# A top-2 router kernel whose first loads are regrouped: logits first, then x in four pieces, and the early store's rows multiplied second

## The chip, the cores and the metric

One core of a Trainium2 chip runs the program. The metric is the device time of one execution in microseconds (us), given as the median of five runs; beside the runs there is one execution taken by the hardware profiler, and all rows quoted below come from that one. Work on the core is done by engines that run independently: here VectorE (DVE) does all the arithmetic, ScalarE (ACT) computes two sigmoids, and 16 DMA engines move data between the device memory (HBM) and the on-chip memory (SBUF, 128 partitions). A DMA is issued by an instruction on SyncE's queue (SPq) or ScalarE's queue (ACTq) and then runs by itself.

## The reference

```python
x: (16, 1024, 512) float32; router_logits: (16, 1024, 8) float32; k = 2
probs = softmax(router_logits)                  # over the 8 experts
topk_probs = the two largest probs, ascending   # (16, 1024, 2)
topk_probs = topk_probs / sum(topk_probs)
out = x[:, :, None, :] * topk_probs[..., None]  # (16, 1024, 2, 512) float32
```

Each of the 16384 tokens is copied twice, scaled by its two normalized weights. The two weights depend only on the difference of the two largest logits: sigmoid(-d) and sigmoid(d). x is 33.6 MB, the logits 0.5 MB and the output 67.1 MB, 101.2 MB in all.

## The kernel before

The 16384 tokens are cut into two groups, of 65 and 63 tokens per partition (`GROUPS`); a "row" below is one token in each of the 128 partitions, so a row of x is 2 KB per partition and 0.26 MB in all, and a row of output twice that. A DMA over n rows is carried as 128 packets, one for each partition, 8 on each of the 16 DMA engines, so the packet is n x 2 KB for a load and n x 4 KB for a store.

There are two big tiles: `xs` holds a whole group of x (65 rows), `osp` holds 16 rows of output. The rest of a group's output is written over rows of `xs` that are no longer needed (`over`). Eight small tiles and `WA` hold the work on the logits.

The order of DMAs on SyncE's queue is the order of the program, and each instruction there waits in line. In group 0 the loads of x (L112) have 2, 2, 4, 8, 17, 28 and 4 rows; behind the first 16 rows stand the two logits loads (L116 for group 0, L117 for group 1), and `top2_weights` (L27 to L43) computes the weights of all 128 rows at once: eleven VectorE instructions over both groups, then two sigmoids on ScalarE. Then come the multiplies (L128), each followed by the store of its rows (L136):

```python
begin = [(0, e, osp[:, :e]), (e, L - e, osp[:, e:])] if g == 0 else [(0, L, osp)]   # e = 2, L = 16
```

In group 0 the multiplies have 2 rows (into `osp`, stored from ScalarE's queue: the "early store", 1 MB), 14 rows (`osp`), 16 rows (over `xs`), 8 and 8 rows (`osp`), 9 and 8 rows (over `xs`); in group 1 16 rows (`osp`), 16 rows (over `xs`), 8, 8 (`osp`) and 15 rows (over `xs`). All stores but the early one are issued on SyncE's queue. A multiply into `osp` waits until the earlier store out of `osp` has landed, and the loads of group 1 wait until the stores out of `xs` have landed. Waits are written by the framework, which also gives each DMA one of eight completion counters in turn; a DMA that reuses a counter waits for that counter's earlier DMA.

The tiles are placed in SBUF in the order in which the program asks for them. In the built program of before `logits` begins at byte 16512 of each partition, `xs` at 20608, `osp` at 153728, and the small tiles follow.

Of the kernel before, what the change touches and what calls it, by code (L numbers as in the profile page):

```python
# [1 line left out]

# [4 lines left out]

F32 = mybir.dt.float32
ALU = mybir.AluOpType
ACTF = mybir.ActivationFunctionType  # L10
P = 128


def top2_weights(nc, pool, logits, M, E):

    hi, lo, n = None, None, E  # L20
    while n > 1:
        n //= 2
        if hi is None:
            a, b = logits[:, :, 0:n], logits[:, :, n : 2 * n]
            nhi = pool.tile([P, M, n], F32, tag=f"hi{n}")
            nlo = b
            nc.vector.tensor_tensor(nhi, a, b, op=ALU.max)  # L27
            nc.vector.tensor_tensor(nlo, a, b, op=ALU.min)  # L28
        else:
            a, b = hi[:, :, 0:n], hi[:, :, n : 2 * n]  # L30
            nhi = pool.tile([P, M, n], F32, tag=f"hi{n}")
            nlo = pool.tile([P, M, n], F32, tag=f"lo{n}")
            tmp = pool.tile([P, M, n], F32, tag=f"tmp{n}")
            nc.vector.tensor_tensor(tmp, lo[:, :, 0:n], lo[:, :, n : 2 * n], op=ALU.max)  # L34
            nc.vector.tensor_tensor(nlo, a, b, op=ALU.min)  # L35
            nc.vector.tensor_tensor(nlo, nlo, tmp, op=ALU.max)  # L36
            nc.vector.tensor_tensor(nhi, a, b, op=ALU.max)  # L37
        hi, lo = nhi, nlo
    dlt = pool.tile([P, M], F32, tag="dlt")
    nc.vector.tensor_tensor(dlt, hi[:, :, 0], lo[:, :, 0], op=ALU.subtract)  # L40
    WA = pool.tile([P, M, 2], F32, tag="WA")
    nc.scalar.activation(WA[:, :, 0], dlt, ACTF.Sigmoid, scale=-1.0)  # L42
    nc.scalar.activation(WA[:, :, 1], dlt, ACTF.Sigmoid, scale=1.0)  # L43
    return WA

GROUPS = [65, 63]

LOADS = [[2, 2, 4, 8, 17, 28, 4], [16, 16, 31]]


LAST = [[(48, 9), (57, 8)], [(48, 15)]]


@with_exitstack
def kernel(
    ctx: ExitStack,
    tc: tile.TileContext,  # L60
    x: bass.AP,
    router_logits: bass.AP,
    k: bass.AP,
    out: bass.AP,
):
    nc = tc.nc
    B, S, D = x.shape
    E = router_logits.shape[-1]
    N = B * S
    assert int(k) == 2 and E == 8 and N == P * sum(GROUPS)  # L70
    M = N // P

    L = 16
    x_v, o_v, rl_v = [], [], []
    t0 = 0
    for n in GROUPS:
        t1 = t0 + P * n
        x_v.append(
            x.rearrange("b s d -> (b s) d")[t0:t1].rearrange("(p m) d -> p m d", p=P)
        )  # L80
        o_v.append(
            out.rearrange("b s k d -> (b s) k d")[t0:t1].rearrange(
                "(p m) k d -> p m k d", p=P
            )
        )
        rl_v.append(
            router_logits.rearrange("b s e -> (b s) e")[t0:t1].rearrange(
                "(p m) e -> p m e", p=P
            )
        )  # L90
        t0 = t1

    wpool = ctx.enter_context(tc.tile_pool(name="wpool", bufs=1))
    logits = wpool.tile([P, M, E], F32)
    xs = wpool.tile([P, max(GROUPS), D], F32)
    osp = wpool.tile([P, L, 2, D], F32)

    def over(r, n, G):

        a = 2 * r - G
        return xs[:, a : a + 2 * n, :].rearrange("p (r k) d -> p r k d", k=2)

    h = L // 2
    e = 2
    m0 = 0
    for g, G in enumerate(GROUPS):
        r = 0  # L110
        for n in LOADS[g]:
            nc.sync.dma_start(xs[:, r : r + n, :], x_v[g][:, r : r + n, :])  # L112
            r += n
            if g == 0 and r == L:

                nc.sync.dma_start(logits[:, :G], rl_v[0])  # L116
                nc.sync.dma_start(logits[:, G:], rl_v[1])  # L117
                WA = top2_weights(nc, wpool, logits, M, E)
        assert r == G
        begin = [(0, e, osp[:, :e]), (e, L - e, osp[:, e:])] if g == 0 else [(0, L, osp)]  # L120
        plan = begin + [
            (L, L, over(L, L, 2 * L)),
            (2 * L, h, osp[:, :h]),
            (2 * L + h, h, osp[:, h:]),
        ]
        plan += [(r, n, over(r, n, G)) for r, n in LAST[g]]
        for r, n, og in plan:
            nc.vector.tensor_tensor(  # L128
                og,
                xs[:, r : r + n, :].unsqueeze(2).to_broadcast([P, n, 2, D]),  # L130
                WA[:, m0 + r : m0 + r + n, :].unsqueeze(3).to_broadcast([P, n, 2, D]),
                op=ALU.mult,
            )

            queue = nc.scalar if n == e else nc.sync
            queue.dma_start(o_v[g][:, r : r + n], og)  # L136
        m0 += G


# [1 line left out]
_INS = ['x', 'router_logits', 'k']  # L141
_OUTS = [((16, 1024, 2, 512), 'float32')]

_NUMBERS = {'k': 2}


# [26 lines left out]
```

## Time and profile before

| quantity | value |
|---|---|
| five runs | 240.53, 240.71, 241.07, 241.88, 241.99 us; median 241.07 |
| profiled execution | 240.49 us, of which the profile's span is 238.7 us |
| VectorE busy | 142.0 us (59% of the span), 23 instructions |
| ScalarE busy | 1.8 us |
| DMA | 3456 packets, 101.19 MB, mean 424 GB/s |
| packet records, first start to last end | 1.74 us to 237.42 us of the span |
| DMA landing times: early store, 14-row store | 23.0 us, 28.0 us after issue |

The trace also records when each DMA packet started and how long it took. The median time of a packet by its size, all from the profiled execution of before:

| bytes | 2016 | 2080 | 4096 | 8192 | 16384 | 32768 | 34816 | 57344 | 65536 |
|---|---|---|---|---|---|---|---|---|---|
| ns | 82 | 85 | 159 | 309 | 611 | 1213 | 1288 | 2116 | 2418 |

Sixteen DMA engines work side by side; a DMA also ends with one 4-byte packet of 9 ns on each engine. To read the views: the busy share of an engine says nothing by itself about what sets the end; the slices show whether the DMA engines ever stand still, and the chain of waits shows what each late step waited for.

### The profile page before, as it was taken

Reading aid. Unit: us, or ns where it says so; the run is one execution under the profiler, and the core shown is the slowest. Engines: PE = TensorE matmul, PEld = TensorE weight load, DVE = VectorE, ACT = ScalarE, POOL = GpSimd, SP = SyncE. Lnnn points to the kernel's source line nnn. Section 1 sums busy time; section 2 is a strip of 40 time slices with the busy share of each in tenths; the row PEclk is TensorE's granted clock in tenths of the full one; section 3 lists DMA queues with packets and bytes.
Section 4 is the critical chain, followed back from the end, with each engine's and each line's share of the span. In section 5 each row is a group of like instructions: output and inputs, shape, how many; then the busy total and the mean of one; then the engine's idle time right before and its main releaser. Section 6 shows DMA issues by size and latency. Waiting matters only on the chain.

```text
span 238.7 us, 118 instructions
## 1 busy us (share of the span) xinstructions
DVE 142.0 (59%) x23; ACT 1.8 (1%) x3; POOL 0.2 (0%) x4
## 2 busy tenths in 40 slices
DVE  0058999990299699910000699999106999990000
ACT  2000000000000000000000000000000000000000
POOL 0000000000000000000000000000000000000000
DMA  7999989999798999999999999998999989999994
GB/s 262 438 464 450 428 367 512 351 461 461 329 527 351 439 439 439 439 395 478 439 428 423 417 489 447 404 505 362 483 395 428 450 373 423 434 439 428 494 484 175
DMA packets 3456, 101.19 MB, mean 424 GB/s; under 512 B 384, under 2 KB 512, under 8 KB 896
## 3 DMA queue, kind: packets, MB, share of 16 engines
q1 hardware_dynamic: 3312, 100.14, 97.7%
q10 hardware_dynamic: 144, 1.05, 1.0%
HBM read 34.08 MB, written 67.11 MB: 424 GB/s over the span
## 4 chain that ended last, share of the span: by engine, by line
DMA 43%; DVE 41%; issue 5%; SPq 1%; ACT 0%; DVEq 0%
DVE xs L128 22%; DVE osp L128 17%; DMA xs<-in_x_dram 13%; DMA out_dram<-osp 13%; DMA out_dram<-xs 13%; DMA logits<-in_router_logits_dram 5%; SPq L112 1%; DVE nhi L27 0%; DVE logits L28 0%; DVE nlo L36 0%; DVE nhi L37 0%; DVE tmp L34 0%; DVE nlo L35 0%; SPq L116 0%; SPq L136 0%
## 5 line engine op out<-in xcount | busy, mean ns | idle before, releaser
L128 DVE TENSOR_TENSOR osp<-xs,WA 128x8192 f32<-128x8192 f32 (+3 forms) x7 | 69.1, 9908 | 56.0 <-DMA xs<-in_x_dram 31.2
L128 DVE TENSOR_TENSOR xs<-xs,WA 128x16384 f32<-128x16384 f32 (+3 forms) x5 | 69.1, 13812 | 2.2 <-DMA out_dram<-xs 2.0
L27 DVE TENSOR_TENSOR nhi<-logits 128x512 f32<-128x512 f32 x1 | 0.7, 693 | 14.4 <-DMA logits<-in_router_logits_dram 14.4
L42 ACT ACT_TABLE_LOAD x1 | 1.3, 1283 | 0.7 <-PEq L154 0.7
L28 DVE TENSOR_TENSOR logits<-logits 128x512 f32<-128x512 f32 x1 | 0.7, 691 | 0.0
L37 DVE TENSOR_TENSOR nhi<-nhi 128x256 f32<-128x256 f32 (+1 forms) x2 | 0.7, 352 | 0.0
L35 DVE TENSOR_TENSOR nlo<-nhi 128x256 f32<-128x256 f32 (+1 forms) x2 | 0.7, 352 | 0.0
L36 DVE TENSOR_TENSOR nlo<-nlo,tmp 128x256 f32<-128x256 f32 (+1 forms) x2 | 0.7, 352 | 0.0
L42 ACT ACTIVATE WA<-dlt 128x128 f32<-128x128 f32 x1 | 0.3, 315 | 16.3 <-DVE dlt L40 16.3
L34 DVE TENSOR_TENSOR tmp<-logits 128x256 f32<-128x256 f32 x1 | 0.4, 417 | 0.0
L40 DVE TENSOR_TENSOR dlt<-nhi,nlo 128x128 f32<-128x128 f32 x1 | 0.3, 292 | 0.0
L43 ACT ACTIVATE WA<-dlt 128x128 f32<-128x128 f32 x1 | 0.3, 298 | 0.0
L34 DVE TENSOR_TENSOR tmp<-nlo 128x128 f32<-128x128 f32 x1 | 0.3, 286 | 0.0
L154 POOL MEMSET const-bfloat16-1.0<- 128x1 bf16 x1 | 0.1, 102 | 0.0
L154 POOL MEMSET const-uint8-127<- 128x1 uint8 x1 | 0.1, 102 | 0.0
L154 POOL MEMSET const-float32-1.0<- 128x1 f32 x1 | 0.1, 99 | 0.0
L154 POOL MEMSET const-float32-0.0<- 128x1 f32 x1 | 0.1, 98 | 0.2 <-issue 0.2
## 6 DMA issues: line engine op xcount, KB each, us to landing
out_dram<-osp SPq DMA_DIRECT2D x4, 4096.0 KB, 20.8
xs<-in_x_dram SPq DMA_DIRECT2D x2, 4096.0 KB, 30.0
xs<-in_x_dram SPq DMA_DIRECT2D x1, 7936.0 KB, 38.1
out_dram<-xs SPq DMA_DIRECT2D x1, 7680.0 KB, 23.2
xs<-in_x_dram SPq DMA_DIRECT2D x1, 7168.0 KB, 39.7
out_dram<-osp SPq DMA_DIRECT2D x1, 7168.0 KB, 28.0
out_dram<-xs SPq DMA_DIRECT2D x1, 4608.0 KB, 20.4
xs<-in_x_dram SPq DMA_DIRECT2D x1, 4352.0 KB, 20.9
```

The source lines that it names most:

```text
L27: nc.vector.tensor_tensor(nhi, a, b, op=ALU.max)
L28: nc.vector.tensor_tensor(nlo, a, b, op=ALU.min)
L34: nc.vector.tensor_tensor(tmp, lo[:, :, 0:n], lo[:, :, n : 2 * n], op=ALU.max)
L35: nc.vector.tensor_tensor(nlo, a, b, op=ALU.min)
L36: nc.vector.tensor_tensor(nlo, nlo, tmp, op=ALU.max)
L37: nc.vector.tensor_tensor(nhi, a, b, op=ALU.max)
L40: nc.vector.tensor_tensor(dlt, hi[:, :, 0], lo[:, :, 0], op=ALU.subtract)
L42: nc.scalar.activation(WA[:, :, 0], dlt, ACTF.Sigmoid, scale=-1.0)
L43: nc.scalar.activation(WA[:, :, 1], dlt, ACTF.Sigmoid, scale=1.0)
L112: nc.sync.dma_start(xs[:, r : r + n, :], x_v[g][:, r : r + n, :])
L128: nc.vector.tensor_tensor(og, xs[:, r : r + n, :].unsqueeze(2).to_broadcast([P, n, 2, D]), WA[:, m0 + r : m0 + r + n, :].unsqueeze(3).to_b ...
L154: nc = _bacc.Bacc("TRN2", target_bir_lowering=False, num_devices=1)
```

## The change

The order of the first instructions is altered and the work on the logits is split by group.

- The logits of group 0 are the first DMA of the program; their weights are computed at once (tags "a").
- x of group 0 is loaded in pieces of 16, 17, 28 and 4 rows (32, 34, 56 and 8 KB per partition) instead of 2, 2, 4, 8, 17, 28 and 4.
- The logits of group 1 are loaded behind the first piece, and their weights are computed apart (tags "b").
- In group 0 the 14 rows are multiplied and stored first, and the 2 rows of the early store second.

```diff
-def top2_weights(nc, pool, logits, M, E):
+def top2_weights(nc, pool, logits, M, E, tag=""):
...
-LOADS = [[2, 2, 4, 8, 17, 28, 4], [16, 16, 31]]
+LOADS = [[16, 17, 28, 4], [16, 16, 31]]
...
-    logits = wpool.tile([P, M, E], F32)
+    logits = wpool.tile([P, sum(GROUPS), E], F32)
+    first, second = logits[:, : GROUPS[0]], logits[:, GROUPS[0] :]
+    nc.sync.dma_start(first, rl_v[0])
+    W = [top2_weights(nc, wpool, first, GROUPS[0], E, "a")]
+
     xs = wpool.tile([P, max(GROUPS), D], F32)
     osp = wpool.tile([P, L, 2, D], F32)
...
-                nc.sync.dma_start(logits[:, :G], rl_v[0])
-                nc.sync.dma_start(logits[:, G:], rl_v[1])
-                WA = top2_weights(nc, wpool, logits, M, E)
+                nc.sync.dma_start(second, rl_v[1])
+                W.append(top2_weights(nc, wpool, second, GROUPS[1], E, "b"))
...
-        begin = [(0, e, osp[:, :e]), (e, L - e, osp[:, e:])] if g == 0 else [(0, L, osp)]
+        begin = [(e, L - e, osp[:, e:]), (0, e, osp[:, :e])] if g == 0 else [(0, L, osp)]
...
-                WA[:, m0 + r : m0 + r + n, :].unsqueeze(3).to_broadcast([P, n, 2, D]),
+                W[g][:, r : r + n, :].unsqueeze(3).to_broadcast([P, n, 2, D]),
```

In the built program VectorE's order is: eleven instructions for the weights of group 0; the 14-row multiply; the first of the eleven for group 1 (L27, which waits for that group's logits); the 2-row multiply; nine more for group 1; the 16-row multiply; the last one (L40); and from the first 8-row multiply on the old order. SyncE's order is: logits of group 0, 16 rows of x, logits of group 1, 17, 28 and 4 rows, and then the stores and loads of before. Because the small tiles "a" are now asked for ahead of `xs`, `xs` begins at byte 24992 and `osp` at 158112: 4384 bytes higher, so that both now begin at an odd multiple of 32 bytes (before: at a multiple of 128).

More of the change, by code (lines that the diff above doesn't have):

```diff
@@ L24, in top2_weights @@
             a, b = logits[:, :, 0:n], logits[:, :, n : 2 * n]
-            nhi = pool.tile([P, M, n], F32, tag=f"hi{n}")
+            nhi = pool.tile([P, M, n], F32, tag=f"hi{n}{tag}")
             nlo = b
@@ L30, in top2_weights @@
             a, b = hi[:, :, 0:n], hi[:, :, n : 2 * n]
-            nhi = pool.tile([P, M, n], F32, tag=f"hi{n}")
-            nlo = pool.tile([P, M, n], F32, tag=f"lo{n}")
-            tmp = pool.tile([P, M, n], F32, tag=f"tmp{n}")
+            nhi = pool.tile([P, M, n], F32, tag=f"hi{n}{tag}")
+            nlo = pool.tile([P, M, n], F32, tag=f"lo{n}{tag}")
+            tmp = pool.tile([P, M, n], F32, tag=f"tmp{n}{tag}")
             nc.vector.tensor_tensor(tmp, lo[:, :, 0:n], lo[:, :, n : 2 * n], op=ALU.max)
@@ L38, in top2_weights @@
         hi, lo = nhi, nlo
-    dlt = pool.tile([P, M], F32, tag="dlt")
+    dlt = pool.tile([P, M], F32, tag=f"dlt{tag}")
     nc.vector.tensor_tensor(dlt, hi[:, :, 0], lo[:, :, 0], op=ALU.subtract)
-    WA = pool.tile([P, M, 2], F32, tag="WA")
+    WA = pool.tile([P, M, 2], F32, tag=f"WA{tag}")
     nc.scalar.activation(WA[:, :, 0], dlt, ACTF.Sigmoid, scale=-1.0)
@@ L70 @@
     assert int(k) == 2 and E == 8 and N == P * sum(GROUPS)
-    M = N // P
     L = 16
@@ L107 @@
     e = 2
-    m0 = 0
     for g, G in enumerate(GROUPS):
@@ L136 @@
             queue.dma_start(o_v[g][:, r : r + n], og)
-        m0 += G
 _INS = ['x', 'router_logits', 'k']
```

## Prediction

> **What bounds the kernel now.** I read the page first: engines, slices, queues.
>
> ```profile
> span 238.7 us, 118 instructions
> DVE 142.0 (59%) x23; ACT 1.8 (1%) x3; POOL 0.2 (0%) x4
> ...
> DMA  7999989999798999999999999998999989999994
> ...
> q1 hardware_dynamic: 3312, 100.14, 97.7%
> q10 hardware_dynamic: 144, 1.05, 1.0%
> ```
>
> VectorE rests 41% of the time, while the two DMA queues together hold the 16 DMA engines for 98.7% of the span; only the first and last slices are visibly short. So the DMA engines are the bound, if they never run out of work. Whether they do is read from the chain of waits and the order of time.
>
> ```profile
> 3.13 11.18 DMA logits<-in_router_logits_dram
> ...
> 53.46 30.06 DMA out_dram<-xs
> ...
> 102.52 30.78 DMA xs<-in_x_dram
> ...
> 150.57 30.51 DMA out_dram<-osp
> ```
>
> Columns: start, length, what. The long waits are all for DMAs that had been issued long before and stood in a queue: a 16-row store of 8.4 MB takes 19.3 us at 434 GB/s (16 engines x 57344 bytes in 2116 ns) but lands after 30. The engines still had 10 us of older work when it was issued.
>
> ```profile
> 21.20 0.37 ACTq L136 DMA_DIRECT2D out_dram<-osp  x1
> 36.20 0.35 SPq L136 DMA_DIRECT2D out_dram<-osp  x1
> 36.21 17.23 DVE L128 TENSOR_TENSOR xs<-xs,WA 128x16384 f32<-128x16384 f32 x1
> 53.46 0.34 SPq L136 DMA_DIRECT2D out_dram<-xs  x1
> 64.29 17.30 DVE L128 TENSOR_TENSOR osp<-xs,WA 128x8192 f32<-128x8192 f32 x2 [10.85 <-DMA out_dram<-osp]
> ...
> 214.69 0.33 SPq L136 DMA_DIRECT2D out_dram<-xs  x1
> ```
>
> Spare time at each store is the landing of the one before minus this issue. The loads of group 0 take the engines to 43 us (packet records); the 14-row store comes at 36.2, 7 us early; it keeps them until it lands at 36.2 + 28.0 = 64.2, the next comes at 53.5, 11 us early. The tightest place is the last store: issued at 214.69, its first packet starts at 218.6, 3.9 us later. Nowhere do the engines run dry.
>
> So I count DMA engine time from the packet records. Each engine's packets at their median durations need 234.30 us; they took 235.81, from 1.74 to 237.42 (neighbours overlap by 0.13). The excess of 1.5 us lies in three places: 0.52 at the start (first 4 KB packets of 200 to 745 ns for 159), 0.15 in the 28-row load, and 0.80 in the 4-row load, whose 8 KB packets ran between 43.2 and 46.9 us at up to 881 ns for 309. Everything after that has 0.03. A change can win at most these plus what it saves in packets, and can lose by new excess or by an empty queue.
>
> **The change, part by part.** The reference time of the sum is the profiled execution, 240.49 us (span 238.7 and 1.8 around it); the median of the runs, 241.07, lies 0.58 above it, so I add 0.58 at the end.
>
> *Fewer pieces.* On each engine 8 packets each of 4, 4, 8 and 16 KB become 8 of 32 KB: 8 x (159 + 159 + 309 + 611) = 9.90 us become 8 x 1.213 = 9.70, a gain of 0.20; three DMAs fewer save three closing packets of 9 ns and their gaps of 6 ns: 0.25 us in all, on the path.
> By the Trainium skill, "DMA: Bandwidth & Descriptors", section "Anatomy of one DMA", a DMA costs about 2.0 us plus its bytes; three DMAs fewer would by that be 6 us. That figure is measured on the other kind of queue. The rows here decide otherwise: DMAs that stand in one queue follow each other within some 15 ns, so only the 0.25 counts.
>
> *Logits first.* The first instruction on SyncE's queue now takes 0.50 us (logits row, L116) instead of 0.38 (first piece of x): first packet 0.12 later. Its 8 packets of 2080 bytes fill each engine for 8 x 85 = 0.68 us, while the next issue takes 0.43: no gap. The starting excess of 0.52 belongs to whichever packets come first; it may be 0.2 less or 0.4 more with other sizes; I take no change.
>
> *Split weights.* Eleven instructions on 128 rows took 14.41 to 18.31, 3.9 us. For half the rows the 0.69 us ones fall to about 0.35 and the rest to between half and all of their 0.20 to 0.34 us steps: 2 to 3 us each time. The first set runs at about 4 us, while x is still on its way, so it costs nothing. The second set stands behind the 14-row multiply; its logits landed near 15 us, so its wait is empty.
>
> *VectorE's new order and the stores.* The first piece ends after 0.27 + 4.19 MB: 1.74 + 0.12 + 0.52 + 4.46/0.434 = 12.7, and it lands about 0.5 later: 13.2. The 14-row multiply (15.1) ends at 28.3, L27 (0.35) and the 2-row multiply (2.3) at 31.0, the rest of the second set at about 33, the 16-row multiply (17.2) at 50. The 14-row store is thus issued at 28.3 instead of 36.2, the early store at 31.0 instead of 21.2, the 16-row store at 50 instead of 53.5. None sets the end: until 43 us the engines have loads, and until about 63 the 14-row store. The cover is 14 us at the first store, 12 at the second; without it each missing microsecond would cost one. Earlier stores gain nothing for the same reason.
>
> *The early store's place.* It is alone on its queue, and in the records its eight packets per engine alternate with the 56 KB packets of the 28-row load, one per 2.4 us: 1 MB lands after 23.0 us. Issued at 31.0, its first packet starts near 35; three go beside the 28-row load, and five beside the 8 KB packets of the 4-row load, all done by about 45. The 8-row multiply that waits for it waits for the 14-row store until 63 anyway. Bytes and order of all later DMAs are the same, and so are their waits: SyncE's later instructions wait for the same stores as before.
>
> *The 4-row load.* Its 0.80 us of excess is the largest known item. It stands in the same place (last load, ahead of the 14-row store), but now with early-store packets in between. Bounds: it goes (-0.8), or it doubles because both kinds of small packet suffer (+0.8). The nearest row is the load itself: I keep it. Mixing alone cost little, 0.15 us over the whole 28-row load.
>
> *The shifted tiles.* `xs` and `osp` begin at an odd multiple of 32 bytes. The one row with such a start is group 1's logits (16512 + 2080): its 2016-byte packets took 82 ns against 85 for 2080 bytes from an even start, in proportion. That shows loads at no cost; no store with such a start is in the trace. I take 0; below nothing is excluded, since nothing becomes more regular; upward see the rivals.
> The same page, section "How a descriptor splits into AXI transactions", says that a transfer off a 256-byte boundary fetches the unused bytes too, in steps of 32 bytes. Both kernels start off such a boundary, by 128 and by 160 bytes; that would be one step more per packet, an estimate of some 0.2 us in all.
>
> Sum: -0.25 + 0.12 + 0 + 0 = -0.13 us, that is 240.36 by the profiled execution and 240.9 by the median. A difference of 0.5%, 1.2 us, is about what a measurement of this kernel can tell from no change, and this lies far inside.
>
> **The rivals.**
> *A, slower: stores from odd 32-byte starts.* Place: every store packet out of `osp` and `xs`, 67.1 MB, 154.6 us of engine time at 434 GB/s. For: no row shows it free; the logits row is a load. Against: that row. Price: if only the fixed 8 ns of a packet doubles (159 ns at 4 KB and 1213 at 32 KB leave 8 at no bytes), 21 DMAs x 8 packets x 8 ns = 1.3 us, about 242.3; each per cent on the stores is 1.5 us. It decides from 0.9%: a 64 KB packet of 2440 ns instead of 2418.
> *B, slightly slower: small packets suffer together.* The 4-row load's excess is about 0.1 us per packet and engine; five early-store packets and a doubled excess give +0.5 to +0.8: 241.6. For: the records of 43 to 47 us. Against: the alternation before cost little.
> *C, faster: the 4-row load's stall was due to the early store's end just before it and goes.* -0.8: 240.1. For: it begins as the early store's last packets end, at 43.3. Against: nothing shows that the one caused the other. With a better start (-0.2) and a low median it passes 0.5%.
> *D, the pieces don't take effect, or the queue runs dry at the start.* The built order shows the new order, and the cover is 14 us: no share of its own.
>
> **How the numbers follow.** Main case 0.55, C 0.20, B 0.15, A 0.10. Of the main case 0.02 falls below -0.5% and 0.03 above; C is half beyond; B passes +0.5% in half, A in nearly all. Faster 0.12, same 0.69, slower 0.19. Range: downward -0.13 - 0.8 - 0.2 = -1.1, upward -0.13 + 0.8 + 0.4 = +1.1, and 0.5 on each side for the median of five, as the runs spread from 240.5 to 242.0: 239.4 to 242.6, which takes in A's lowest price.
>
> **What would show it.** Right: first multiply at 13 us, stores at 28, 31 and 50, first 8-row multiply within 1 us of 64.3, slices full in between, and the same waits afterwards, all shifted alike. Wrong: a longer 64 KB packet or a mean rate from 64 to 236 us more than 1% below the 431 GB/s of before (A); the 8-row multiply late by over a microsecond (B) or early by one (C); any empty slice between 3 and 236 us.

## The result and the profile after

The changed kernel takes 240.51 us (median of 54 runs, 240.29 to 241.29) beside 240.73 for the kernel before (94 runs, 240.21 to 242.71): ratio 0.9973, 95% interval 0.9962 to 0.9984. That is 0.27% less, between the forecast's two bounds of 0.5%. The ratio goes with the means, 240.55 and 241.20 us; the medians differ by 0.09%. The profiled execution went from 240.49 to 240.44 us.

The medians hide what moved. The times of before fall in two clusters: 55 of 94 runs at 240.2 to 241.2 (median 240.47) and 39 at 241.3 to 242.7 (the expectations below count 56 and 38). The changed kernel has all its 54 runs in the lower one, at 240.51. So in the lower cluster the change gained nothing; the ratio comes from the missing upper one (39 of 94 runs, on average 1.7 us later, make 0.7 us of the mean). Both clusters are among the undisturbed runs that the comparison uses.

The page of the changed kernel, engines, slices and queues:

```profile
span 238.6 us, 126 instructions
...
DVE 142.7 (60%) x34; ACT 2.1 (1%) x5; POOL 0.2 (0%) x4
...
DMA  8999799999798999999999999898989999999994
...
q1 hardware_dynamic: 2880, 100.14, 97.7%
q10 hardware_dynamic: 144, 1.05, 1.0%
```

432 packets fewer, and the same 98.7% of 16 engines' span. Its chain of waits (start, length, what):

```profile
1.15 12.22 DMA xs<-in_x_dram
...
49.92 33.42 DMA out_dram<-xs
...
102.37 30.63 DMA xs<-in_x_dram
...
150.37 30.50 DMA out_dram<-osp
```

The first wait is now for the first piece of x, no longer for the logits; the 16-row store, issued 3.5 us earlier, waits 3.4 us longer; from 102 us on the chain is the old one, 0.15 to 0.3 us earlier, while the last packet ends 0.11 us earlier (237.31 us for 237.42). In order of time:

```profile
13.47 15.09 DVE L129 TENSOR_TENSOR osp<-xs,WA 128x14336 f32<-128x14336 f32 x1 [7.59 <-DMA xs<-in_x_dram]
...
28.59 0.35 SPq L137 DMA_DIRECT2D out_dram<-osp  x1
...
31.12 0.37 ACTq L137 DMA_DIRECT2D out_dram<-osp  x1
...
49.92 0.34 SPq L137 DMA_DIRECT2D out_dram<-xs  x1
...
64.14 17.29 DVE L129 TENSOR_TENSOR osp<-xs,WA 128x8192 f32<-128x8192 f32 x2 [14.11 <-DMA out_dram<-osp]
...
214.41 0.33 SPq L137 DMA_DIRECT2D out_dram<-xs  x1
```

The first big store comes 7.6 us earlier, and the first 8-row multiply only 0.15: the stores waited in the queue. The DMA engines never rest: in the packet records of this kernel and of every run below, 13 or more packets are under way at every moment from 3 to 236 us, 16 on average.

### The profile page after: what moved, and what is told of

The parts are those of the page before. It is cut to its first block, busy times and chain, and to the rows that moved or that the text cites. A ratio compares the mean times of both kernels' runs of the same rounds, so it can differ in the third digit from the quotient of the medians.

```text
span 238.6 us, 126 instructions
## 1 busy us (share of the span) xinstructions
DVE 142.7 (60%) x34; ACT 2.1 (1%) x5; POOL 0.2 (0%) x4
## 3 DMA queue, kind: packets, MB, share of 16 engines
q10 hardware_dynamic: 144, 1.05, 1.0%
## 4 chain that ended last, share of the span: by engine, by line
DMA 45%; DVE 41%; issue 4%; SPq 0%; DVEq 0%
DVE xs L129 22%; DVE osp L129 18%; DMA xs<-in_x_dram 18%; DMA out_dram<-xs 14%; DMA out_dram<-osp 13%; SPq L95 0%; DVE nlo L35 0%; DVE nhi L37 0%; DVE tmp L34 0%; DVE nlo L36 0%; SPq L137 0%; DVE logits L28 0%; DVE nhi L27 0%; DVEq L129 0%; DVE dlt L40 0%
## 5 line engine op out<-in xcount | busy, mean ns | idle before, releaser
L27 DVE TENSOR_TENSOR nhi<-logits 128x260 f32<-128x260 f32 (+1 forms) x2 | 0.8, 421 | 3.4 <-DMA logits<-in_router_logits_dram 3.4
L37 DVE TENSOR_TENSOR nhi<-nhi 128x130 f32<-128x130 f32 (+3 forms) x4 | 1.0, 255 | 0.0
L36 DVE TENSOR_TENSOR nlo<-nlo,tmp 128x130 f32<-128x130 f32 (+3 forms) x4 | 1.0, 254 | 0.0
L35 DVE TENSOR_TENSOR nlo<-nhi 128x130 f32<-128x130 f32 (+3 forms) x4 | 1.0, 253 | 0.0
L42 ACT ACTIVATE WA<-dlt 128x65 f32<-128x65 f32 (+1 forms) x2 | 0.5, 260 | 47.6 <-DVE dlt L40 47.6
L28 DVE TENSOR_TENSOR logits<-logits 128x260 f32<-128x260 f32 (+1 forms) x2 | 0.8, 421 | 0.0
L34 DVE TENSOR_TENSOR tmp<-logits 128x130 f32<-128x130 f32 (+1 forms) x2 | 0.6, 288 | 0.0
L43 ACT ACTIVATE WA<-dlt 128x65 f32<-128x65 f32 (+1 forms) x2 | 0.5, 244 | 0.0
L40 DVE TENSOR_TENSOR dlt<-nhi,nlo 128x65 f32<-128x65 f32 (+1 forms) x2 | 0.4, 224 | 0.0
```

## The experiments

For each kernel the packet records give three numbers. "Nominal" is the sum of the packets at the median durations that their sizes have in before, per DMA engine; "excess" is what they took above it; and the last packet's end is given for the median one of the 16 engines and for the slowest.

| kernel | nominal us | excess us | work us | median engine ends | slowest ends | this execution, us |
|---|---|---|---|---|---|---|
| before | 234.30 | 1.50 | 235.81 | 237.0 | 237.4 | 240.49 |
| before, again (e5) | 234.30 | 1.45 | 235.75 | 237.0 | 237.5 | 240.44 |
| changed | 234.08 | 1.55 | 235.62 | 236.9 | 237.3 | 240.44 |
| changed, again (e9) | 234.08 | 1.68 | 235.75 | 237.1 | 237.5 | 240.67 |
| e1 four pieces alone | 234.08 | 1.85 | 235.92 | 237.1 | 238.5 | 241.67 |
| e2 order alone | 234.30 | 1.79 | 236.09 | 237.2 | 237.7 | 240.59 |
| e3 address alone | 234.30 | 1.61 | 235.92 | 237.1 | 237.7 | 240.63 |
| e4 logits first alone | 234.30 | 2.43 | 236.74 | 238.1 | 239.0 | 241.99 |
| e6 changed, old order | 234.08 | 1.56 | 235.64 | 236.8 | 237.8 | 240.96 |
| e7 changed, old pieces | 234.30 | 2.04 | 236.34 | 237.5 | 238.9 | 241.79 |
| e8 changed, old address | 234.08 | 1.63 | 235.71 | 236.9 | 237.7 | 240.82 |
| e10 no early store | 234.01 | 1.87 | 235.88 | 237.2 | 238.2 | 241.38 |
| e11 no 8 KB piece | 234.01 | 1.80 | 235.81 | 237.1 | 237.4 | 240.55 |
| e12 neither | 233.95 | 2.00 | 235.95 | 237.2 | 237.7 | 240.78 |

The time of an execution is the slowest engine's end plus 2.9 to 3.2 us in every row; the median engine's end does not give it.

The kernels ran on three chips, e1 to e4 on the first, e5 to e8 on the second and e9 to e12 on the third, each beside runs of before on the same chip. Before had 14 of 35 runs above 241.3 on the first, none of 29 on the second and 2 of 33 on the third: whether there is an upper cluster depends on the chip or the occasion.

### One part alone, on the kernel before (first chip)

**e1: four pieces.**

```diff
-LOADS = [[2, 2, 4, 8, 17, 28, 4], [16, 16, 31]]
+LOADS = [[16, 17, 28, 4], [16, 16, 31]]
```

> The kernel before with the four-piece loads (16, 17, 28, 4 rows) alone; logits still behind the first piece, weights of both groups at once, 2 rows multiplied first, tiles at their old addresses. The 94 runs of before fall in two clusters, 56 at 240.2 to 241.1 us and 38 at 241.3 to 242.7; the 54 of the changed kernel in one, 240.3 to 241.3. Theory P (the prediction's packet sum): 0.25 us less than before in the lower cluster, no say on the clusters. Theory S (the upper cluster comes from the small first packets): all runs in one cluster at 240.2 to 241.1, ratio about 0.997. Theories Q (it comes from the order of the first two multiplies and the early store) and G (from the logits' place and the joint weights): still two clusters, ratio 0.999 to 1.000.

Measured: median 240.93, ratio 0.9993 (0.9963 to 1.0023). Ten of twelve runs at 240.67 to 241.12, against 240.53 as the lower cluster's median of before on this chip, and two at 241.67 and 242.87. Fewer packets alone bring no gain: the excess before 5 us grew from 0.47 to 0.66 us, and the 4-row load's stayed (0.85). The Trainium skill's 2 us for each DMA ("DMA: Bandwidth & Descriptors", "Anatomy of one DMA") does not add up over DMAs here: with three DMAs fewer the lower cluster's median is 240.90, 0.37 us later and not 6 us earlier. Its profiled execution is the one of 241.67, and shows what this late run is made of: the median engine is on time, the slowest 1.47 behind, having lost 0.67 by the end of group 0's loads and 0.62 during the last load of group 1 (one 63488-byte packet of 3061 ns for 2342). That is theory W (stated with e5 below). e10's profiled execution, 241.38, is late in the same way, with its slowest engine 0.95 behind. No late run of before itself was profiled.

**e2: the 14 rows first.**

```diff
-        begin = [(0, e, osp[:, :e]), (e, L - e, osp[:, e:])] if g == 0 else [(0, L, osp)]
+        begin = [(e, L - e, osp[:, e:]), (0, e, osp[:, :e])] if g == 0 else [(0, L, osp)]
```

> The kernel before with the 14 rows multiplied and stored first and the 2 rows of the early store second, all else as before. Theory Q: one cluster at 240.2 to 241.1, ratio about 0.997. Theories S and G: two clusters, ratio 0.999 to 1.000. Theory P: no change, since the cover by queued loads is 7 us or more; the early store then lands near 55 us beside the 14-row store and the first 8-row multiply still starts within 1 us of 64.3.

Measured: median 240.59, ratio 0.9984 (0.9953 to 1.0016), two of twelve runs above 241.3. The early store was issued at 36.3 us, and its packets ran from 41.4 to 46.6; the 8-row multiply began at 64.29, as before. So theory P's "no change" held, but its 55 us for the early store did not. The excess left the 4-row load and came back on the last packets of the 28-row load (0.91 us, one packet of 3131 ns for 2116).

**e3: big tiles at an odd multiple of 32 bytes.**

```diff
+    pad = wpool.tile([P, 8], F32)
+    nc.gpsimd.memset(pad, 0.0)
     xs = wpool.tile([P, max(GROUPS), D], F32)
```

> The kernel before with a 32-byte tile placed ahead of x's tile, so that both big tiles begin at an odd multiple of 32 bytes, as in the changed kernel. Rival A of the prediction: 1.3 us or more slower (ratio above 1.005), 64 KB store packets above 2440 ns. If the start address costs nothing, as the changed kernel's 431 GB/s from 64 to 236 us says: ratio 1.000, two clusters.

Measured: median 240.66, ratio 0.9989 (0.9955 to 1.0023), two of twelve above 241.3; the 64 KB store packets take 2418 ns, as before. The windows view from 64 to 236 us, of this kernel (span, busy times, clock, DMA share, GB/s):

```profile
64.00:236.00 172.00, 103.64 (x9) 0.00 (x0) 0.00 (x0) 1.00 1.00 431
```

The same 431 GB/s as in the changed kernel, whose line is the same, and as before:

```profile
64.00:236.00 172.00, 103.65 (x9) 0.00 (x0) 0.00 (x0) 1.00 1.00 431
```

Rival A is out.

**e4: logits first, weights apart.** The diff is that of the change without its `LOADS` and `begin` lines, with `xs` and `osp` asked for ahead of the weights.

> The kernel before with the first group's logits as the first DMA and the weights computed apart for each group; x still in 2, 2, 4, 8, 17, 28, 4 rows, the 2 rows multiplied first, the big tiles at their old addresses. Theory G: one cluster at 240.2 to 241.1, ratio about 0.997. Theories S and Q: two clusters, ratio 0.999 to 1.000. Theory P: the early store is issued near 8 us instead of 21, no change in time, since the DMA engines have loads until 43 us either way.

Measured: median 241.57, ratio 1.0020 (0.9991 to 1.0048); the fastest run has 241.04, 0.8 above the fastest of before. Theory P's "no change" fails here. The weights are ready at 6.4 us, the first 2 rows have landed, and the early store goes out at 8.8 us, among the first loads of x:

```profile
6.47 2.29 DVE L128 TENSOR_TENSOR osp<-xs,WA 128x2048 f32<-128x2048 f32 x1 [0.47 <-ACT WA L43]
8.79 0.37 ACTq L136 DMA_DIRECT2D out_dram<-osp  x1
```

The packets between 5 and 14 us then have 1.33 us of excess per engine; before had 0.05. The excess is not on the store's packets: 0.62 us is on loads that started before the store was issued, 0.67 on loads that started before its first packet at 12.6 us, and the store's own packets take their 309 ns each. Nothing later explains it either: between 20 and 48 us this kernel has no excess at all. What slows the loads here is not shown.

Of the four parts, each alone has a ratio whose interval includes 1, and each still has runs above 241.3: two of twelve in e1, e2 and e3, and ten of twelve in e4, which is later as a whole. None removes the late runs altogether.

### One part undone, on the changed kernel (second chip)

**e5: the kernel before again.** Its code is unchanged.

> The kernel before once more, for a second profiled execution and more runs beside the others of this call. All theories: two clusters, about 60% of the runs at 240.2 to 241.3 and 40% above. Theory W (the time is that of the slowest of the 16 DMA engines): if the profiled execution falls into the upper cluster, the median engine finishes its last packet near 237.1 us as in the first profile, and one engine 1.5 to 2 us later, having fallen behind during loads. Theory U (all engines stall alike): the median engine itself is 1.5 to 2 us later.

Measured: median 240.47 (240.15 to 240.75, 11 runs), ratio 1.0001 (0.9992 to 1.0010): one cluster, for it and for the 29 runs beside it. The upper cluster was not there to be profiled, so W and U stay untested by this run.

**e6: the 2 rows first again** (the `begin` line of e2, reversed).

> The changed kernel with the 2 rows multiplied and stored first again; logits first, weights apart, four-piece loads as changed. Theory Q (the late place of the early store removes the upper cluster): some of the runs return above 241.3, a fifth to two fifths. Theories S and G: none above 241.3. Theory P: no change against the changed kernel, 240.5 in the lower cluster.

Measured: median 240.40, ratio 1.0012 (0.9995 to 1.0028); nine of eleven runs at 240.26 to 240.96, two at 241.74 and 242.17, while before had none above 240.84. The early store was issued at 16.2 us. In the profiled execution the median engine ends at 236.8 and the slowest 1.0 later, 0.66 of it lost by 26 us. That would speak for Q, but only with two runs, and before, whose early store is early too, has no run above 241.3 among its 40 on this chip.

**e7: the small first pieces again** (the `LOADS` line of e1, reversed).

> The changed kernel with x in 2, 2, 4, 8, 17, 28 and 4 rows again; logits first, weights apart and the 14 rows first as changed. Theory S (small first packets make the upper cluster): runs return above 241.3, and the lower cluster is 0.25 us higher by the packet sum. Theories Q and G: no run above 241.3.

Measured: median 241.37 (241.03 to 241.79, six runs), ratio 1.0042 (1.0030 to 1.0055): 1.0 us, four times the packet sum. Its timeline shows why:

```profile
6.49 2.29 DVE L129 TENSOR_TENSOR osp<-xs,WA 128x2048 f32<-128x2048 f32 x1 [0.47 <-ACT WA L43]
8.81 0.37 ACTq L137 DMA_DIRECT2D out_dram<-osp  x1
...
16.99 15.09 DVE L129 TENSOR_TENSOR osp<-xs,WA 128x14336 f32<-128x14336 f32 x1 [8.21 <-DMA xs<-in_x_dram]
```

Although the program names the 14 rows first, the framework built the 2-row multiply ahead, as soon as its 2 rows were there. So the early store stands among the small loads, as in e4, and the excess is the same: 1.38 us from 5 to 14 us, 0.44 of it on loads that started before the store was issued and 0.93 on loads that started before its first packet at 13.1. In the changed kernel the first 16 rows come in one piece, so that a store can be ready at 16 us at the earliest (e6), and with the 14 rows first at 28. What e7 undid was therefore the pieces and the order together. Before has the small pieces without this excess, and the changed kernel the early logits without it; only the two together show it. A kernel with both and no early store would say what part the store has; none was run.

**e8: the old addresses.**

```diff
     logits = wpool.tile([P, sum(GROUPS), E], F32)
+    xs = wpool.tile([P, max(GROUPS), D], F32)
+    osp = wpool.tile([P, L, 2, D], F32)
     first, second = logits[:, : GROUPS[0]], logits[:, GROUPS[0] :]
```

> The changed kernel with the two big tiles asked for ahead of the weights, so that they stand at their old addresses (multiples of 128 bytes); all else as changed. If the start address plays no part: as the changed kernel, all runs at 240.3 to 241.3. If the odd start is what removes the upper cluster: a fifth to two fifths of the runs above 241.3.

Measured: median 240.68 (240.45 to 241.27), ratio 1.0012 (1.0004 to 1.0021), no run above 241.3. On this chip before has no upper cluster either, so this says nothing on whether the start address removes it. It says only that the changed kernel is no faster than before at the old addresses either: it stands 0.1% above before.

### The stall in the last loads (third chip)

**e9: the changed kernel again.** Its code is unchanged.

> The changed kernel once more, beside the others of this call. Theory W (the time is that of the slowest of the 16 DMA engines, and the change saves 0.2 us on each of them but does not hold the slowest back): the median engine ends near 236.9 us of the span, the slowest 0.4 to 0.6 later, 240.3 to 240.9 in nearly all runs. Where before shows one cluster here, the ratio is 0.999 to 1.002; where it shows two, 0.996 to 0.998. The rival that the change is a gain by itself (fewer packets on the path): 0.25 us under before in any case, ratio 0.999 also without an upper cluster.

Measured: median 240.67 (240.34 to 240.94), ratio 1.0006 (0.9995 to 1.0017), beside 33 runs of before with only two above 241.3. The median engine ends at 237.1 us and the slowest 0.4 later, near theory W's 236.9 and 0.4 to 0.6. Where the upper cluster is rare, the change is no gain. That decides against the rival of a gain by itself.

**e10: no early store; e11: no 8 KB piece; e12: neither.**

```diff
-        begin = [(e, L - e, osp[:, e:]), (0, e, osp[:, :e])] if g == 0 else [(0, L, osp)]
+        begin = [(0, L, osp)]                      # e10, e12
-LOADS = [[16, 17, 28, 4], [16, 16, 31]]
+LOADS = [[16, 17, 32], [16, 16, 31]]               # e11, e12
```

> The changed kernel without the early store: the first 16 rows are multiplied at once and stored by one DMA on SyncE's queue, issued near 31 us. Theory M (the stall of about 0.9 us per engine in group 0's last loads comes from early-store packets beside the loads): excess between 20 and 48 us under 0.2 us per engine, all engines 0.7 us earlier, 239.8. Theory T (it comes at the passage from loads to the first big store): 0.8 to 0.95 remain, 240.5. Theory N (it belongs to the 8 KB load piece): remains, 240.5.

> The changed kernel with x of group 0 in three pieces, 16, 17 and 32 rows, so that no 8 KB load packets are left; the early store as changed. Theory N: excess between 20 and 48 us under 0.2 us per engine, 239.8. Theories M and T: 0.8 to 0.95 remain, 240.5; with the packet sum 0.03 less.

> The changed kernel with both: three pieces of 16, 17 and 32 rows and no early store. Theory T: 0.8 to 0.95 us of excess between 20 and 48 us remain, 240.4. Theories M and N, or both together: excess under 0.2, 239.7, faster than both kernels by 0.3%.

Measured: 240.93 (ratio 1.0017, 0.9998 to 1.0037), 240.78 (1.0017, 1.0008 to 1.0027) and 240.81 (1.0024, 1.0011 to 1.0037). The stall is there in all three, between 40 and 44 us: 1.11 us of excess on the 8 KB packets without the early store, 1.05 on the last 64 KB load packets without the small piece, 1.29 with neither. M and N fall; T, the passage from the loads to the first big store, is what is left of the three. That is by elimination only, and T is not the whole answer: e4 and e7 make the same passage with no excess between 20 and 48 us. The hoped-for faster version does not exist here: e12 has the least nominal work of all and is 0.24% slower than before. Above 241.3 are 3 of 10, 1 of 12 and 2 of 11 runs.

The excess takes back what the packets save. Group 0's loads and the early store are done, for the median engine, at 46.4 to 46.6 us in before, changed, e1, e2, e3, e5, e6, e8 and e9, whatever the pieces. Of these nine executions the four with the small first pieces end their loads at 46.58 us on average and the five with four pieces at 46.54: of the 0.22 us saved, 0.04 is left. The time is 44.3 in e10 and e12, which lack the early store's 1.05 MB (2.4 us at 434 GB/s). Only e4 and e7 are later, 47.1 and 47.0.

## Why the prediction was right, and where its steps were not

The forecast of no clear change was right for its main reason: the DMA engines stay full and every store has cover. That the sum of -0.13 us came so near to nothing is partly luck, since both of its terms were wrong and with opposite signs. The measured 0.27% is not that sum either: it comes from the upper cluster.

- **The bound and the cover: right.** The 16 DMA engines are full in every kernel; the 14-row store came at 28.6 us (28.3 forecast), the early store at 31.1 (31.0), the 16-row store at 49.9 (50), the 8-row multiply at 64.1, and nothing later depended on them. The second set of weights cost VectorE about 2 us and the end nothing.
- **Fewer pieces, -0.25 us: the size failed.** The packets' nominal sum fell by 0.22, but none of it reached the time. Changed and e9 have 235.62 and 235.75 us of work, before and e5 235.81 and 235.75; the median engine ends at 236.9 and 237.1 against 237.0 and 237.0. In all eight comparisons with coarse first pieces (changed, e1, e6, e8 to e12) the median of the runs up to 241.3 lies above that of before beside them, by 0.04 to 0.37 us. The step took the excess as a fixed amount on top; instead the loads end at nearly the same time whatever the pieces.
- **Logits first, +0.12 us: wrong.** The issue took 0.37 us, not 0.50, and the first packet came at 1.72 instead of 1.74. The 0.50 belonged to an issue further back in the line.
- **The 4-row load's 0.80 us: the amount stayed, the place did not.** In the changed kernel its packets take 309 ns each with early-store packets between them, no excess at all, and the 28-row load's last packets take 0.94 us more instead, one up to 3178 ns. So rival B (both kinds of small packet suffer) and rival C (the stall goes) are both out. The prediction never asked what early logits do where x still comes in small pieces: 1 us, with a store among the loads (e4, e7).
- **The shifted tiles, 0: right** (e3). Rival A's price was too high for its place: it counted all 21 DMAs, where the stores it names are 12, or 0.8 us. The one step more per packet of the Trainium skill's "How a descriptor splits into AXI transactions" ("DMA: Bandwidth & Descriptors") shows in no packet duration here.
- **The sum: the wrong engine.** It added up the mean of 16 engines, and the end is set by the slowest, 0.3 to 1.5 us behind the median one. The overlap of 0.13 us that it read sets the mean engine's work against the slowest one's end, so it is no overlap of packets. The spread of the runs was put into the range as noise of the median; in truth the runs fall in two clusters, and the whole measured gain lies in that.

What made the upper cluster go is not settled. It has been profiled in no run of before. The changed kernel has none in 54 and 11 runs; e8, the changed kernel at the old addresses, none in 12. With the 2 rows first again (e6) 2 of 11 were above 241.3, and each part alone (e1, e2, e3) left 2 of 12 beside 14 of 35 of before. That could point to the parts together, early store late and loads coarse. But e8 and e9 ran where before had few late runs or none, and e10 to e12, with coarse loads and a late early store or none, have 6 of 33 late beside 2 of 33 of before. The numbers are small and the chips differ.

## What to carry to other kernels

When all DMA engines are full, regrouping transfers moves little: before counting saved packets, ask whether the phase ends at a time of its own, as these loads did at 46.5 us. Read the end from the slowest engine and look at all runs, since a difference of medians can be a difference in how often a late run occurs. A part that is harmless in company can cost alone: logits first cost 1 us with the small loads, where it also made the early store ready among them, and nothing with the 16-row first piece; and look at the built order, since the framework need not keep the program's.

## What the runs showed of the hardware

- A DMA packet takes 8 ns plus its bytes at 27 GB/s, from 2 KB (82 ns) to 64 KB (2418 ns), and queued DMAs follow each other within some 15 ns.
- Near the end of group 0's loads, ahead of the first big store, load packets take 0.5 to 1.3 us longer per engine in all but e4 and e7, on 8 KB, 56 KB or 64 KB packets alike. In e4 and e7 there is no excess there, and 1.3 to 1.4 us at 5 to 14 us, nearly all on loads ahead of the early store's first packet. At the passage from group 1's loads (160 us) it is 0.01 to 0.3 us. Why the first passage costs more, and why it costs nothing in e4 and e7, was not found.
- Stores hardly spread the engines: the slowest engine's lag behind the median one changes during loads and stays the same within 0.02 us through the big stores (0.67 us from 47 to 123 us in e1).
- Big tiles at an odd multiple of 32 bytes in SBUF instead of 128 cost nothing measurable, for loads and stores (e3: ratio 0.9989, 0.9955 to 1.0023; 64 KB packets of 2418 ns in both).
